# Twelve seven-product pairs instead of ten in the down projection, three of them with weight sums made during the up projection

## The chip, the core and the metric

The kernel runs on one core of a Trainium2 chip. The time is the device time of one execution in microseconds (us). Of this kernel before the change there are three timed runs, 1303.25 to 1303.45 us, median 1303.36, and one further execution taken with the profiler. The engines have short names below: PE multiplies matrices, DVE and ACT work element by element, POOL and SP only issue transfers in the stages that matter here.

## The reference

One layer of an encoder trunk on 256 positions with a width of 2048, all in float32. The change is in the last part, the gated feed-forward network with 5504 hidden channels:

```python
def conv_ffn(x, g_norm, w_up, conv_k, conv_b, w_down):
    h = rms_norm(x, g_norm)
    up = h @ w_up
    ...
    up = (pad[:, :t] * conv_k[0] + pad[:, 1:t + 1] * conv_k[1]
          + pad[:, 2:t + 2] * conv_k[2] + conv_b)
    gate, val = jnp.split(up, 2, axis=-1)
    return x + (jax.nn.silu(gate) * val) @ w_down
```

Ahead of it stand the two mixer branches, their merge and an output projection; behind it a last RMS norm.

## The kernel before

**Precision.** PE gets each float32 operand as a high and a low part. A weight piece is loaded as `wraw`, ACT copies its rounded high part to `whi` (L153), and DVE subtracts it to get the low part `wlo` (L154). This is called a split below. A product of two split operands is three matmuls, high by high, low by high, high by low; `triple` writes them (L291 to L293).

**Order of work.** The weights are a list of pieces. `begin(i)` stands ahead of the matmuls of piece i: it issues loads up to piece i + 4 (five `wraw` buffers), the splits up to piece i + 3 (four `whi` and `wlo` buffers), and then the tasks that `at(i, ...)` left for piece i. Every engine takes its own instructions in the written order, and semaphores do the rest.

**Up projection.** A group is eight pieces of 256 contraction rows by 512 columns: the columns are two blocks of 128 gate channels and two of the matching value channels. PE runs 64 matmuls with `whi` (L205) and 64 with `wlo` (L209) for it. While the next group runs, `ev_up` adds the two halves of each result bank (`tb`, `ta`), makes the convolution and the gate, and splits the result into the activation tile `a`. Two blocks of 128 channels form one contraction pair of the down projection, so group p leaves pair p. There are 21 whole pairs and a last single block.

**Down projection.** It runs twice, for columns 0 to 1023 (g = 0) and 1024 to 2047 (g = 1), each with 43 pieces of 128 rows by 1024 columns. Two pieces are a pair q. A plain pair takes eight triples: two row blocks, two column blocks, two halves of the contraction. For the pairs in `DOWN_QUADS` a scheme with seven products is used instead (`run_wide`): three triples at the first piece (r = 0) and four at the second (r = 1), with sums of weight blocks and sums of activation blocks as operands. The four weight sums, `t13` and `t24`, are made by four DVE additions (`weight_sums`, at piece i - 3 for a pair that begins at piece i) and split at i - 2 (`weight_sums_split`: two ACT copies, two DVE subtractions into `h13`, `l13`, `h24`, `l24`). The split sums have two sets of buffers that take turns, one in `hpool`, one in a pool `twice` (`both_rooms`). The activation sums of a pair are made while the up projection runs, `sums` and `sums_split` of `ev_up`, stored to device memory by POOL (L1029), and read back by `stored` at piece i - 4 (L1194) into one of two buffers.

Ten pairs per g are such pairs: pairs 3, 5, 7, 9, 10, 12, 14, 16, 17 and 19 of the contraction, which stand at those places for g = 0 and at 2, 4, 6, 8, 9, 11, 13, 14, 16 and 18 for g = 1. The seven-product pair needs whole `wraw` pieces for its sums, but of its own two pieces only one and a half are split.

**Tail.** The last four pieces of g = 1 are run block by block, so that the final norm and the stores of one block lie beside the products of the next.

Of the kernel before, what the change touches and what calls it, by code (L numbers as in the profile page):

```python
# [8 lines left out]
F32 = mybir.dt.float32  # L9
# [48 lines left out]
TURN_X2 = (13, 1)  # L58
Y_GAP = 224
PAD = 16  # L60
DOWN_PAIRS = (3, 5, 7, 9, 10, 12, 14, 16, 17, 19)
DOWN_QUADS = (DOWN_PAIRS, (2, 4, 6, 8, 9, 11, 13, 14, 16, 18))


@with_exitstack
def trunk_kernel(ctx, tc, x, x_t, vecs, w_in, ln_g, ln_b, w_st, b_s, rpb, w_branch, w_out, w_up, w_down,
# [17 lines left out]
    wpool = keep("weights")  # L84
    tmp = keep("tmp")
    hpool = keep("hT")
    ypool, y_st = pool("yT", "right")

    junk = tmp.tile([128, 512], F32, name="junk")
# [17 lines left out]
        return first  # L107

    raw, split_t = {}, {}
    whole, units = {}, {}  # L110
    n_loaded = [0]
    n_split = [0]

    def load_to(n):
        while n_loaded[0] < min(n, len(pieces)):
            i = n_loaded[0]
            n_loaded[0] += 1
            if i in preload:
                for f in preload[i]:
                    f()  # L120
            src, r0, kn, (c0, cn, nb, cs), step = pieces[i]
            w = wpool.tile([128, 2, 512], F32, name="wraw", bufs=LOAD_AHEAD)
# [15 lines left out]
            raw[i] = w  # L138
            if i in whole:
                whole[i] = w  # L140
# [31 lines left out]
    def at(i, f):  # L172
        tasks.setdefault(i, []).append(f)
# [90 lines left out]

    def wide(src, row0, order, c0, acts, quads, room, done, sums=None, stored=None, split_room=None):
        n0 = plan_wide(src, row0, order, c0)
        boxes = {}
        for q in quads:  # L270
            i = n0 + 2 * q
            own = split_room or room
            whole[i] = whole[i + 1] = None
            units[i], units[i + 1] = 1, 2
            b = boxes[q] = {}
            if stored:
                b["acts"] = {}
                at(i - 4, lambda b=b, k=order[2 * q]: stored(k // 2, b["acts"]))
            else:
                b["acts"] = sums[order[2 * q]]  # L280
# [51 lines left out]
    def weight_sums_split(box, room):  # L332
        u = []
        for name, t in zip(("13", "24"), box.pop("w")):
            h, l = room("h" + name, F32R), room("l" + name, F32R)
            nc.scalar.activation(h, t, AF.Copy)  # L336
            nc.vector.tensor_sub(l, t, h.bitcast(F32))
            u.append((h, l))
        box["t"] = {1: [x[:, 0] for x in u[0]], 3: [x[:, 1] for x in u[0]],
                    2: [x[:, 1] for x in u[1]], 4: [x[:, 0] for x in u[1]]}  # L340

# [282 lines left out]
    def combine(ps):  # L624
        outs = []
        bs = []
        for p in ps:
            t = tmp.tile([128, T], F32, name="tb", bufs=3)
            nc.scalar.activation(t, p[:, T:], AF.Copy)
            a = tmp.tile([128, T], F32, name="ta", bufs=6)  # L630
            nc.vector.tensor_add(a, p[:, :T], t)
            outs.append(a)
        return outs
# [353 lines left out]
    def ev_up(f0, nb):  # L987
        def done(ps, i):
            n = nb
            a = []  # L990
            own = {}
            for p in ps:
                t = tmp.tile([128, T], F32, name="tb", bufs=3)
                nc.scalar.activation(t, p[:, T:], AF.Copy)
                u = tmp.tile([128, T], F32, name="ta", bufs=6)
                nc.vector.tensor_add(u, p[:, :T], t)
                a.append(u)

            def conv(b):
                c = []  # L1000
                for u, ch in ((a[b], f0 + b), (a[n + b], NF + f0 + b)):
                    nc.vector.tensor_mul(u, u, rs["rb"])  # L1002
                    v = ff["p"].tile([128, T], F32, name="tc", bufs=4)
                    nc.scalar.activation(v, u, AF.Identity, scale=ck[:, 1, ch:ch + 1], bias=ck[:, 3, ch:ch + 1])  # L1004
                    c.append((u, v, ch))
                for u, v, ch in c:
                    nc.vector.scalar_tensor_tensor(v[:, 1:], u[:, :T - 1], ck[:, 0, ch:ch + 1], v[:, 1:],  # L1007
                                                   op0=OP.mult, op1=OP.add)
                    nc.vector.scalar_tensor_tensor(v[:, :T - 1], u[:, 1:], ck[:, 2, ch:ch + 1], v[:, :T - 1],
                                                   op0=OP.mult, op1=OP.add)  # L1010
# [173 lines left out]
    def down_room(name, dt):  # L1184
        return hpool.tile([128, 2, 512], dt, name=h_room[name])

    def both_rooms(name, dt):
        n = ff[name] = ff.get(name, -1) + 1
        return (ff["twice"] if n % 2 else hpool).tile([128, 2, 512], dt, name=h_room[name])

    def stored(pair, box):
        n = ff["turn"] = ff.get("turn", -1) + 1
        o = down_room(f"s{n % 2}", F32R)
        nc.gpsimd.dma_start(o.bitcast(F32), ff["kept"][pair])  # L1194
        box["s"] = sums_of(o)

    def down_order(g):
        free = [p for p in range(NF // 2) if p not in DOWN_PAIRS]
# [2 lines left out]
        return tuple(2 * p + kk for p in pairs for kk in range(2)) + (NF - 1,)  # L1201

    g_dn = [wide(w_d, 0, down_order(g), g * 1024, lambda k: ff["a"][k], DOWN_QUADS[g], down_room,
                 (ev_sums(2 * g, down_room), ev_down if g == 0 else finish), stored=stored, split_room=both_rooms) for g in range(2)]
    ff["kept"] = {p: dram.tile([128, 2, 512], F32, name=f"sums{p}") for p in DOWN_PAIRS}

    first_chunk = X_TURN[1][0]
    preload[2] = [lambda: load_xt(2 * first_chunk, 1)]
# [85 lines left out]
    s_room["st"].close()  # L1294
    for half in (1, 0):
        mg["m_st", half].close()
    fa, fa_st = pool("act")
    ctx.push(fa_st)
    ff["ap"] = [fa.tile([128, min(2, NF - k), 2, T], F32R, name=f"a{k // 2}") for k in range(0, NF, 2)]
    ff["a"] = [ff["ap"][k // 2][:, k % 2] for k in range(NF)]  # L1300
    ff["more"], more_st = pool("more")
    fc = {}

# [5 lines left out]
        run_group(g)  # L1309
    def open_twice():  # L1310
        more_st.close()
        ff["twice"], twice_st = pool("twice")
        ctx.push(twice_st)

# [60 lines left out]
```

## Time and profile before

| | |
|---|---|
| median of three runs | 1303.36 us |
| profiled execution | 1303.95 us, its span 1302.2 us |
| granted clock of PE | 0.999 of full speed |
| busy: PE, DVE, ACT, POOL | 99%, 83%, 60%, 8% |
| DMA | 280.34 MB, mean 215 GB/s |
| first matmul of the down projection | 1073.20 us from the span's start |

The time and the span of the profiled execution differ by 1.75 us, which lie outside the profile. A row of a timeline has the start, the duration, the engine, the line and the operation, out<-in, and in brackets how long the engine stood idle just before and what ended that. Rows in time order can be merged (x and a count). The rows of grouped instructions have the busy time and the mean duration in ns behind the bar. PE's matmuls overlap: a row's duration is longer than the distance from one start to the next.

### The profile page before, as it was taken

To read this page: it belongs to the slowest core of one execution; us is meant where nothing else is said; L and a number is where in the kernel's file an instruction comes from. 1 tells how busy PE (TensorE), PEld (TensorE's weight loads), DVE (VectorE), ACT (ScalarE), POOL (GpSimd) and SP (SyncE) were. 2 spreads that over 40 slices of the span, in tenths; PEclk is the share of its full clock that TensorE was granted. 3 is DMA by queue.
4 is the path that set the end of the run, shared out by engine and by line. 5 is a ranking of instruction groups with operands and counts; after the bars stand their busy time and mean duration, and the time that the engine had idled before them with its cause. 6 is when DMAs were issued, how large, how long until landed. Compare 5 with 4: busy or idle time off the path is not lost.

```text
span 1302.2 us, 19268 instructions
## 1 busy us (share of the span) xinstructions
PE 1291.6 (99%) x6703; PEld 1102.0 (85%) x6703; DVE 1078.2 (83%) x1620; ACT 780.2 (60%) x1156; POOL 108.9 (8%) x212
## 2 busy tenths in 40 slices
PE   9999999999999999999999999999999999999997
PEld 7888888888888888888888888888888888888886
DVE  7896777677689988997778878787878889999997
ACT  7765576676655645566555556565655656655564
POOL 0006405413000000000000000000000000000000
PEclk9999999999999999999999999999999999999999
DMA  9789656566566667665566666666666658876883
GB/s 368 268 275 251 199 164 210 178 165 191 178 213 224 200 188 249 202 212 173 172 202 196 189 213 196 210 195 216 188 211 200 211 157 293 292 268 222 271 285 112
DMA packets 174513, 280.34 MB, mean 215 GB/s; under 512 B 13392, under 2 KB 121552, under 8 KB 174416
## 3 DMA queue, kind: packets, MB, share of 16 engines
q1 hardware_dynamic: 164944, 251.89, 60.1%
q0 software_dynamic: 8896, 26.17, 6.5%
q8 instruction: 52, 0.85, 0.3%
q10 hardware_dynamic: 576, 1.06, 0.2%
q14 instruction: 45, 0.37, 0.1%
HBM read 268.05 MB, written 8.91 MB: 213 GB/s over the span
## 4 chain that ended last, share of the span: by engine, by line
PE 99%; DVE 1%; ACT 0%; issue 0%; POOL 0%; POOLq 0%; ACTq 0%
PE bank L205 31%; PE bank L209 16%; PE bank L291 12%; PE bank L293 12%; PE bank L292 12%; PE bank L233 4%; PE bank L234 4%; PE bank L235 4%; PE bank L777 1%; PE bank L827 0%; PE bank L906 0%; PE bank L642 0%; PE bank L978 0%; PE bank L817 0%; PE bank L450 0%
## 5 line engine op out<-in xcount | busy, mean ns | idle before, releaser
L154 DVE TENSOR_TENSOR wlo<-wraw,whi 128x1024 fp32r<-128x1024 f32 (+1 forms) x472 | 545.4, 1170 | 174.1 <-ACT whi L153 93.1
L153 ACT ACTIVATE whi<-wraw 128x1024 fp32r<-128x1024 f32 (+1 forms) x472 | 470.0, 1009 | 213.0 <-PE bank L292 75.2
L205 PE MATMUL bank<-h,whi 128*128 128x512 f32 x1760 | 425.8, 392 | 0.6 <-DVE ya L646 0.6
L205 PEld LDWEIGHTS bank<-h,whi 128*128 128x128 f32 x1760 | 322.0, 188 | 62.7 <-DVE ya L646 1.0
L209 PEld LDWEIGHTS bank<-h,wlo 128*128 128x128 f32 x1760 | 225.9, 191 | 8.8
L209 PE MATMUL bank<-h,wlo 128*128 128x256 f32 x1760 | 228.6, 283 | 0.0
L1004 ACT ACTIVATE tc<-ta,ck 128x256 f32<-128x256 f32 x86 | 47.1, 594 | 117.1 <-DVE ta L1002 117.1
L293 PE MATMUL bank<-wlo,a 128*128 128x512 f32 x224 | 87.3, 390 | 0.0
L292 PE MATMUL bank<-whi,a 128*128 128x512 f32 x224 | 87.2, 389 | 0.0
L291 PE MATMUL bank<-whi,a 128*128 128x512 f32 x224 | 87.1, 389 | 0.0
L291 PE MATMUL bank<-whi,h 128*128 128x512 f32 x210 | 82.2, 391 | 0.0
L293 PE MATMUL bank<-wlo,h 128*128 128x512 f32 x210 | 82.1, 391 | 0.0
L292 PE MATMUL bank<-whi,h 128*128 128x512 f32 x210 | 81.8, 389 | 0.0
L336 ACT ACTIVATE h<-h 128x1024 fp32r<-128x1024 f32 x40 | 40.2, 1053 | 34.3 <-DVE h L328 34.3
L1007 DVE SCALAR_TENSOR_TENSOR tc<-ta,ck,tc 128x255 f32<-128x255 f32 x86 | 41.4, 481 | 14.5 <-ACT tc L1004 14.5
L1029 POOL DMA_DIRECT2D sums<-so x10 | 5.4, 538 | 548.1 <-DVE so L494 459.8
L233 PE MATMUL bank<-whi,y 128*128 128x512 f32 x128 | 50.5, 394 | 0.0
L233 PE MATMUL bank<-whi,h 128*128 128x512 f32 x128 | 50.4, 394 | 0.0
L235 PE MATMUL bank<-wlo,h 128*128 128x512 f32 x128 | 49.9, 390 | 0.0
L235 PE MATMUL bank<-wlo,y 128*128 128x512 f32 x128 | 49.9, 390 | 0.0
L234 PE MATMUL bank<-whi,h 128*128 128x512 f32 x128 | 49.8, 389 | 0.0
L234 PE MATMUL bank<-whi,y 128*128 128x512 f32 x128 | 49.8, 389 | 0.0
(285 smaller groups left out, 1833.2 us busy)
## 6 DMA issues: line engine op xcount, KB each, us to landing
wraw<-in_w_up_dram SPq DMA_DIRECT2D x336, 256.0 KB, 3.2
wraw<-in_w_in_dram SPq DMA_DIRECT2D x111, 512.0 KB, 4.6
wraw<-in_w_down_dram SPq DMA_DIRECT2D x86, 512.0 KB, 5.3
wraw<-in_w_in_dram SPq DMA_DIRECT2D x66, 256.0 KB, 3.3
wraw<-in_w_branch_dram SPq DMA_DIRECT2D x32, 512.0 KB, 4.5
wraw<-in_w_out_dram SPq DMA_DIRECT2D x32, 512.0 KB, 4.5
h<-sums POOLq DMA_DIRECT2D x20, 512.0 KB, 6.4
sums<-so POOLq DMA_DIRECT2D x10, 512.0 KB, 4.2
```

Source lines behind the costliest of these rows:

```text
L153: nc.scalar.activation(h[:, k, :m], w[:, k, :m], AF.Copy)
L154: nc.vector.tensor_sub(l[:, k, :m], w[:, k, :m], h[:, k, :m].bitcast(F32))
L205: nc.tensor.matmul(p, h[:, k - k0, b * 128:(b + 1) * 128], acts(k), start=k == 0, stop=k == nk - 1)
L209: nc.tensor.matmul(p[:, :T], l[:, k - k0, b * 128:(b + 1) * 128], acts(k)[:, 0, :], start=False, stop=False)
L233: nc.tensor.matmul(p, xh, h[:, kk, :m], start=st, stop=False)
L234: nc.tensor.matmul(p, xl, h[:, kk, :m], start=False, stop=False)
L235: nc.tensor.matmul(p, xh, l[:, kk, :m], start=False, stop=sp)
L291: nc.tensor.matmul(p, xh, h, start=st, stop=False)
L292: nc.tensor.matmul(p, xl, h, start=False, stop=False)
L293: nc.tensor.matmul(p, xh, l, start=False, stop=sp)
L1004: nc.scalar.activation(v, u, AF.Identity, scale=ck[:, 1, ch:ch + 1], bias=ck[:, 3, ch:ch + 1])
L1007: nc.vector.scalar_tensor_tensor(v[:, 1:], u[:, :T - 1], ck[:, 0, ch:ch + 1], v[:, 1:], op0=OP.mult, op1=OP.add)
```

## The change

Two more pairs of each half use seven products, twelve in place of ten. The lists of places are new: 3, 5, 6, 7, 9, 11, 12, 13, 15, 17, 18, 19 for g = 0 and 2, 4, 5, 6, 8, 10, 11, 12, 14, 16, 17, 18 for g = 1.

For the pairs 6, 12 and 18 the weight sums are not made in the down projection. `split_ahead` makes them during the up projection, once for each pair and g, so six times, beginning at the groups 2, 5, 9, 11, 15 and 17: POOL loads the 1 MB of weights at the first piece of that group into `tw`, DVE makes the four additions at its last two pieces and at the first two of the next group, and ACT and DVE split the sums at the third and fifth piece of the next group. The high parts go through the buffer `so`, which the activation sums also use and of which there is one; the low parts replace the sums in `tw`. POOL stores the four tiles of 512 KB to device memory. In the down projection `split_read` reads the four tiles back, at piece i - 6, into one set of buffers in `twice`. Such a pair makes no sums in the down projection, and of its first weight piece only half the columns are loaded.

The nine other pairs of each half make their split sums in `hpool` alone, in one set of buffers. The activation sums have a third buffer, `s2`, in `twice`. The tiles `ta` and `tb` move from the pool `tmp`, open for the whole kernel, to pools of their own, the second of which closes ahead of `twice` and lies where `twice` comes to lie.

```diff
-DOWN_PAIRS = (3, 5, 7, 9, 10, 12, 14, 16, 17, 19)
-DOWN_QUADS = (DOWN_PAIRS, (2, 4, 6, 8, 9, 11, 13, 14, 16, 18))
+DOWN_PAIRS = (3, 5, 6, 7, 9, 11, 12, 13, 15, 17, 18, 19)
+DOWN_QUADS = (DOWN_PAIRS, (2, 4, 5, 6, 8, 10, 11, 12, 14, 16, 17, 18))
+SPLIT_PAIRS = (6, 12, 18)
+SPLIT_IN = ((2, 5), (9, 11), (15, 17))
...
+            if i in halved:
+                kn = 1
...
+            if split and k // 2 in SPLIT_PAIRS:
+                halved.add(i)
+                at(i - 6, lambda b=b, k=k: split(k // 2, b))
+                continue
+            whole[i] = whole[i + 1] = None
             at(i - 3, lambda i=i, b=b: weight_sums(i, b, room))
-            at(i - 2, lambda b=b, own=own: weight_sums_split(b, own))
+            at(i - 2, lambda b=b: weight_sums_split(b, room))
...
-    def both_rooms(name, dt):
-        n = ff[name] = ff.get(name, -1) + 1
-        return (ff["twice"] if n % 2 else hpool).tile([128, 2, 512], dt, name=h_room[name])
-
     def stored(pair, box):
-        n = ff["turn"] = ff.get("turn", -1) + 1
-        o = down_room(f"s{n % 2}", F32R)
+        n = ff["turn"] = (ff.get("turn", -1) + 1) % 3
+        o = ff["twice"].tile([128, 2, 512], F32R, name="s2") if n == 2 else down_room(f"s{n}", F32R)
         nc.gpsimd.dma_start(o.bitcast(F32), ff["kept"][pair])
         box["s"] = sums_of(o)
+
+    def split_read(g):
+        def read(pair, box):
+            u = []
+            for n in ("13", "24"):
+                u.append([ff["twice"].tile([128, 2, 512], F32R, name=p + n) for p in "hl"])
+                for t, src in zip(u[-1], t_kept[pair, g][n]):
+                    nc.gpsimd.dma_start(t.bitcast(F32), src)
+            split_sums(box, u)
+        return read
+
+    def split_ahead(pair, g, i):
+        box = {}
+
+        def load():
+            w = box["w"] = ff["more"].tile([128, 4, 512], F32, name="tw")
...
+        def add(d, a, b):
+            w = box["w"]
+            nc.vector.tensor_add(w[:, d], w[:, a], w[:, b])
+
+        def split(c, n):
+            w = box["w"][:, c:c + 2]
+            h = ff["more"].tile([128, 2, 512], F32R, name="so")
+            low = w.bitcast(F32R)
+            nc.scalar.activation(h, w, AF.Copy)
+            nc.vector.tensor_sub(low, w, h.bitcast(F32))
+            for dst, v in zip(t_kept[pair, g][n], (h.bitcast(F32), w)):
+                nc.gpsimd.dma_start(dst, v)
+
+        at(i, load)
+        for n, (d, a, b) in enumerate(((0, 0, 1), (1, 1, 3), (3, 0, 3), (2, 2, 3))):
+            at(i + 6 + n, lambda d=d, a=a, b=b: add(d, a, b))
+        at(i + 10, lambda: split(0, "13"))
+        at(i + 12, lambda: split(2, "24"))
...
+    turns["p"], turns_st = pool("turns2")
     ff["more"], more_st = pool("more")
...
     def open_twice():
         more_st.close()
+        turns_st.close()
         ff["twice"], twice_st = pool("twice")
```

The first place is DVE in the up projection, from the second piece's split on after group 11 has ended. The kernel before has there:

```order
L154 TENSOR_TENSOR wlo_8814<-wraw_8791,whi_8813 128x1024
L1002 TENSOR_TENSOR ta_8777<-ta_8777,rb_6196 128x256
L1002 TENSOR_TENSOR ta_8785<-ta_8785,rb_6196 128x256
L1007 SCALAR_TENSOR_TENSOR tc_8818<-ta_8777,ck_88,tc_8818 128x255
L1009 SCALAR_TENSOR_TENSOR tc_8818<-ta_8777,ck_88,tc_8818 128x255
L1007 SCALAR_TENSOR_TENSOR tc_8821<-ta_8785,ck_88,tc_8821 128x255
L1009 SCALAR_TENSOR_TENSOR tc_8821<-ta_8785,ck_88,tc_8821 128x255
L154 TENSOR_TENSOR wlo_8855<-wraw_8810,whi_8854 128x1024
L1015 TENSOR_TENSOR tc_8818<-tc_8818,tc_8821 128x256
```

The changed kernel has at that place, on DVE, where `tw` holds the weights of one pair ahead and `so` their high parts:

```order
L1227 TENSOR_TENSOR tw_8647<-tw_8647 128x512
L160 TENSOR_TENSOR wlo_8900<-wraw_8876,whi_8899 128x1024
L1227 TENSOR_TENSOR tw_8647<-tw_8647 128x512
L1015 TENSOR_TENSOR ta_8862<-ta_8862,rb_6229 128x256
L1015 TENSOR_TENSOR ta_8870<-ta_8870,rb_6229 128x256
L1020 SCALAR_TENSOR_TENSOR tc_8905<-ta_8862,ck_91,tc_8905 128x255
L1022 SCALAR_TENSOR_TENSOR tc_8905<-ta_8862,ck_91,tc_8905 128x255
L1020 SCALAR_TENSOR_TENSOR tc_8908<-ta_8870,ck_91,tc_8908 128x255
L1022 SCALAR_TENSOR_TENSOR tc_8908<-ta_8870,ck_91,tc_8908 128x255
L160 TENSOR_TENSOR wlo_8942<-wraw_8896,whi_8941 128x1024
L1234 TENSOR_TENSOR tw_8647<-tw_8647,so_8945 128x1024
L1028 TENSOR_TENSOR tc_8905<-tc_8905,tc_8908 128x256
```

Two additions and the subtraction of a split ahead (L1227, L1234) stand between the splits of the up projection's own pieces (L160, L154 before) and the convolution.

The second place is POOL at the start of the down projection. The kernel before reads the activation sums of pairs 3 and 5, two parts of the last norm's weight, and the sums of pairs 7 and 9:

```order
L1194 DMA h6_11135<-sums3_123 128x1024
L1194 DMA h7_11231<-sums5_124 128x1024
L1329 DMA gfin_11237<-in_norm_final_dram 128x512
L1329 DMA gfin_11239<-in_norm_final_dram 128x512
L1194 DMA h6_11328<-sums7_125 128x1024
L1194 DMA h7_11413<-sums9_126 128x1024
```

The changed kernel has on POOL there:

```order
L1203 DMA h6_11282<-sums3_126 128x1024
L1203 DMA h7_11379<-sums5_127 128x1024
L1212 DMA h13_11381<-h13_6_0_138 128x1024
L1212 DMA l13_11382<-l13_6_0_139 128x1024
L1212 DMA h24_11385<-h24_6_0_140 128x1024
L1212 DMA l24_11386<-l24_6_0_141 128x1024
L1385 DMA gfin_11393<-in_norm_final_dram 128x512
L1385 DMA gfin_11395<-in_norm_final_dram 128x512
L1203 DMA s2_11448<-sums6_128 128x1024
L1203 DMA h6_11486<-sums7_129 128x1024
```

The four tiles of pair 6 (L1212) and its activation sums have come in ahead of the sums of pair 7.

More of the change, by code (lines that the diff above doesn't have):

```diff
@@ L86, in trunk_kernel @@
     hpool = keep("hT")
+    turns, turns_st = pool("turns")
+    turns = {"p": turns}
     ypool, y_st = pool("yT", "right")
@@ L109, in trunk_kernel @@
     raw, split_t = {}, {}
-    whole, units = {}, {}
+    whole, units, halved = {}, {}, set()
     n_loaded = [0]
@@ L262, in run_group, with wide @@
             done(ps, b)
-    def wide(src, row0, order, c0, acts, quads, room, done, sums=None, stored=None, split_room=None):
+    def wide(src, row0, order, c0, acts, quads, room, done, sums=None, stored=None, split=None):
         n0 = plan_wide(src, row0, order, c0)
@@ L271, in wide @@
             i = n0 + 2 * q
-            own = split_room or room
-            whole[i] = whole[i + 1] = None
+            k = order[2 * q]
             units[i], units[i + 1] = 1, 2
@@ L277, in wide @@
                 b["acts"] = {}
-                at(i - 4, lambda b=b, k=order[2 * q]: stored(k // 2, b["acts"]))
+                at(i - 4, lambda b=b, k=k: stored(k // 2, b["acts"]))
             else:
-                b["acts"] = sums[order[2 * q]]
+                b["acts"] = sums[k]
+            if split and k // 2 in SPLIT_PAIRS:
[3 more added lines that the diff above has]
+            whole[i] = whole[i + 1] = None
             at(i - 3, lambda i=i, b=b: weight_sums(i, b, room))
-            at(i - 2, lambda b=b, own=own: weight_sums_split(b, own))
+            at(i - 2, lambda b=b: weight_sums_split(b, room))
         return ("wide", n0, order, acts, quads, boxes, done)
@@ L627, in combine @@
         for p in ps:
-            t = tmp.tile([128, T], F32, name="tb", bufs=3)
+            t = turns["p"].tile([128, T], F32, name="tb", bufs=3)
             nc.scalar.activation(t, p[:, T:], AF.Copy)
-            a = tmp.tile([128, T], F32, name="ta", bufs=6)
+            a = turns["p"].tile([128, T], F32, name="ta", bufs=6)
             nc.vector.tensor_add(a, p[:, :T], t)
@@ L992, in done @@
             for p in ps:
-                t = tmp.tile([128, T], F32, name="tb", bufs=3)
+                t = turns["p"].tile([128, T], F32, name="tb", bufs=3)
                 nc.scalar.activation(t, p[:, T:], AF.Copy)
-                u = tmp.tile([128, T], F32, name="ta", bufs=6)
+                u = turns["p"].tile([128, T], F32, name="ta", bufs=6)
                 nc.vector.tensor_add(u, p[:, :T], t)
@@ L1203, in trunk_kernel @@
     g_dn = [wide(w_d, 0, down_order(g), g * 1024, lambda k: ff["a"][k], DOWN_QUADS[g], down_room,
-                 (ev_sums(2 * g, down_room), ev_down if g == 0 else finish), stored=stored, split_room=both_rooms) for g in range(2)]
+                 (ev_sums(2 * g, down_room), ev_down if g == 0 else finish), stored=stored, split=split_read(g)) for g in range(2)]
     ff["kept"] = {p: dram.tile([128, 2, 512], F32, name=f"sums{p}") for p in DOWN_PAIRS}
+    t_kept = {}
+    for p, turn in zip(SPLIT_PAIRS, SPLIT_IN):
+        for g in range(2):
+            t_kept[p, g] = {n: [dram.tile([128, 2, 512], F32, name=f"{h}{n}_{p}_{g}") for h in "hl"]
+                            for n in ("13", "24")}
+            split_ahead(p, g, g_up[turn[g]][1])
     first_chunk = X_TURN[1][0]
```

6 lines of the change are left out of this document (added).

## The prediction

> **What bounds the kernel now.** I read the page first, then the waits of PE's weight loads, then a table of stages.
>
> ```profile
> PE 1291.6 (99%) x6703; PEld 1102.0 (85%) x6703; DVE 1078.2 (83%) x1620; ACT 780.2 (60%) x1156; POOL 108.9 (8%) x212
> PE 99%; DVE 1%; ACT 0%; issue 0%; POOL 0%; POOLq 0%; ACTq 0%
> PEld bank L293 <- DVE wlo L154: 0.3, 1, 0.3
> 706.31:1020.00 313.69, 313.69 (x1802) 277.12 (x1801) 254.88 (x436) 184.36 (x291) 4.82 (x9) 1.00 0.65 203
> 1080.00:1280.00 200.00, 200.00 (x884) 165.62 (x883) 190.96 (x228) 119.17 (x136) 11.72 (x22) 1.00 0.78 264
> ```
>
> The first two lines are the page's busy times and its chain of waits: both are PE. The third is the whole list of PE's waits in the down projection, one wait of 0.3 us for DVE. The last two are stages of the up and the down projection: length, busy time of PE, its loads, DVE, ACT and POOL, granted clock, DMA share, GB/s. DVE is busy 254.88 of 313.69 us (81%) in the first and 190.96 of 200 us (95%) in the second. So PE sets the time everywhere, but in the down projection DVE is almost a second bound, and an edit that only added seven-product pairs would soon be DVE's.
>
> How fast PE goes there is seen in the timeline, with the stage's first and last matmul around one triple:
>
> ```profile
> 1073.20 0.39 PE L291 MATMUL bank<-whi,a 128*128 128x512 f32 x1
> ...
> 1104.00 0.39 PE L291 MATMUL bank<-h,a 128*128 128x512 f32 x1
> 1104.23 0.39 PE L292 MATMUL bank<-h,a 128*128 128x512 f32 x1
> 1104.46 0.39 PE L293 MATMUL bank<-h,a 128*128 128x512 f32 x1
> 1104.68 0.39 PE L291 MATMUL bank<-whi,a 128*128 128x512 f32 x1
> ...
> 1293.52 0.39 PE L293 MATMUL bank<-wlo,a 128*128 128x512 f32 x1
> ```
>
> A triple starts every 0.68 us (1104.68 - 1104.00), a matmul every 0.227, though each row lasts 0.39. By the code there are 2 x (10 x 7 + 11.5 x 8) = 324 triples, 220.3 us; the rows give 1293.52 + 0.23 - 1073.20 = 220.5. So nothing but issue is in this stage, and what follows it, the tail to 1302.2, is 8.5 us.
>
> **PE's saving.** Each new seven-product pair drops one triple. Two more per half are four triples, 12 matmuls: 4 x 0.68 = 2.72 us. That is all the change can take from this path; nothing that it removes elsewhere was waited for.
>
> **DVE in the down projection.** Its costs, by form, in the stage's groups:
>
> ```profile
> L154 DVE TENSOR_TENSOR wlo<-wraw,whi 128x1024 fp32r<-128x1024 f32 x61 | 73.3, 1221 | 7.6 <-ACT whi L153 7.6
> L337 DVE TENSOR_TENSOR h<-h,h 128x1024 fp32r<-128x1024 f32 x40 | 47.1, 1221 | 0.0
> L327 DVE TENSOR_TENSOR h<-h,wraw 128x512 f32<-128x512 f32 x20 | 13.8, 692 | 0.7
> L154 DVE TENSOR_TENSOR wlo<-wraw,whi 128x512 fp32r<-128x512 f32 x20 | 13.8, 688 | 0.2 <-ACT whi L153 0.2
> ```
>
> The other three additions are taken like L327, 0.69 us. A pair with its sums made here costs 4 x 0.69 + 2 x 1.22 + 1.22 + 0.69 = 7.11 us of DVE against 7 x 0.68 = 4.76 of PE; a plain pair 2.44 against 5.44; a pair that is read back 1.91 against 4.76. From place 3 to 19 of the first half, before: DVE 10 x 7.11 + 7 x 2.44 = 88.2, PE 85.7. After: 9 x 7.11 + 3 x 1.91 + 5 x 2.44 = 81.9, PE 12 x 4.76 + 5 x 5.44 = 84.3. DVE goes from behind PE to ahead of it, and two costly pairs are never neighbours any more. Price: 0.
>
> **One set of buffers.** The copies of the next costly pair must now wait for PE's last product of the one before. The timeline has both, for the pairs at places 12 and 14:
>
> ```profile
> 1139.82 0.39 PE L293 MATMUL bank<-h,a 128*128 128x512 f32 x1
> 1140.19 2.01 ACT L336 ACTIVATE h<-h 128x1024 fp32r<-128x1024 f32 x2 [1.83 <-DVE h L328]
> ```
>
> With two sets, ACT already begins only when the last of these matmuls is ending, held by DVE's sums; behind it on ACT are the splits of the next pieces. At worst the wait adds about 0.02 us to that start (1139.82 + 0.39 - 1140.19), and PE gets to these sums 7.5 us later (two plain pieces and r = 0, 11 triples). Below nothing it cannot go, since PE was not waiting; above, the 7.5 less ACT's 1.05 and DVE's 2.44 leave some 4 us of cover. Price 0.
>
> **Reading back.** 2 x 3 x 4 tiles of 512 KB come in on POOL's queue beside the weights. The tightest place is the first, pair 6:
>
> ```profile
> 1083.56 0.48 DVE L1009 SCALAR_TENSOR_TENSOR tc<-ta,ck,tc 128x255 f32<-128x255 f32 x1
> 1098.85 2.35 DVE L337 TENSOR_TENSOR h<-h,h 128x1024 fp32r<-128x1024 f32 x2
> 1101.96 0.39 PE L291 MATMUL bank<-h,h 128*128 128x512 f32 x1
> 1102.97 0.63 ACT L153 ACTIVATE whi<-wraw 128x512 fp32r<-128x512 f32 x1 [1.83 <-DMA wraw<-in_w_down_dram]
> 1076.00:1084.00 8.00, 8.00 (x36) 6.41 (x35) 7.59 (x15) 5.37 (x10) 0.00 (x0) 1.00 1.01 400
> 1084.00:1090.00 6.00, 6.00 (x28) 4.95 (x28) 5.97 (x10) 3.66 (x6) 1.08 (x2) 1.00 0.76 244
> 1090.00:1106.00 16.00, 16.00 (x72) 13.27 (x71) 15.78 (x19) 9.17 (x11) 1.07 (x2) 1.00 0.82 274
> h<-sums POOLq DMA_DIRECT2D x20, 512.0 KB, 6.4
> ```
>
> The tiles lie where `ta` lay, so they start when the last convolution has read it, 1084.05. PE wants them at 1104.68 + 2.04 = 1106.7. In those 22 us DMA moved 6 x 244 + 16 x 274 = 5.85 MB; new are 4 x 0.524 + 0.524 (the sums of pair 6) - 0.262 (the half piece) = 2.36 MB: 8.2 MB. At 400 GB/s, which the stage just ahead shows at a full DMA share, 22 us carry 8.8 MB. It fits, but at first in a heap: if the 2.36 and 0.5 MB of the norm's weight come within 11 us beside 270 GB/s of weights, about 1.1 MB are left over, 2.7 us by which a weight piece is late. ACT waits for a piece there already (1.83). Cover: the low parts of pair 5 begin at 1098.85, the first is done at 1100.07 and PE needs it at 1101.96 + 0.45: 2.3 us; and a piece is requested several us ahead of its split. Nothing can be gained, since PE has no wait there; lost can be 2.7 - 2.3 = 0.4 us, and 0.4 + 0.68 at pair 7, whose products now begin a triple earlier: 1.5 us. I take 0, since the pieces' own lead comes on top of the cover. The later reads start as soon as the previous read-back pair is done, some ten pieces ahead, where DVE is no tighter.
>
> The row for capacity is 400 GB/s. The Trainium skill, HBM Reference, Specifications, gives about 425 GB/s for a core that streams alone and 358 for its share when both cores of a pair do. By 358 the 22 us would carry 7.9 MB, 0.3 MB too few, under 1 us late; one core runs here and the row is above that share, so the trace speaks for the first figure.
>
> **The up projection.** Six times DVE gets 4 x 0.69 + 2 x 1.22 = 5.2 us, ACT 2 x 1.05, POOL one load and four stores. The stage has 59 us of DVE idle in the 314 above, against 31 in all; what counts is one group. For one, DVE's idle places, ACT's splits, and PE's high products (12, then 7 behind the low ones, one every 0.23 us):
>
> ```profile
> 818.91 1.23 DVE L154 TENSOR_TENSOR wlo<-wraw,whi 128x1024 fp32r<-128x1024 f32 x1 [0.47 <-ACT whi L153]
> 821.95 1.23 DVE L154 TENSOR_TENSOR wlo<-wraw,whi 128x1024 fp32r<-128x1024 f32 x1 [1.81 <-PE bank L209]
> 837.74 1.23 DVE L154 TENSOR_TENSOR wlo<-wraw,whi 128x1024 fp32r<-128x1024 f32 x1 [0.54 <-PE bank L209]
> ...
> 824.54 1.05 ACT L153 ACTIVATE whi<-wraw 128x1024 fp32r<-128x1024 f32 x1
> ...
> 830.42 1.04 ACT L153 ACTIVATE whi<-wraw 128x1024 fp32r<-128x1024 f32 x1
> ...
> 831.68 1.04 ACT L153 ACTIVATE whi<-wraw 128x1024 fp32r<-128x1024 f32 x1
> ...
> 833.78 2.91 PE L205 MATMUL bank<-h,whi 128*128 128x512 f32 x12
> ...
> 838.44 1.78 PE L205 MATMUL bank<-h,whi 128*128 128x512 f32 x7
> ```
>
> The group's last piece has its high part at 831.46, and PE begins with it after eight of the 12, at 835.62: 4.2 us of cover. The next group's first piece has 832.72 against 838.44 + 4 x 0.23 = 839.36: 6.6 us. Of the change, DVE does one addition in the group's first piece and one in its second, 1.22 us in its third and fifth. The first addition falls into the 1.81 us. The second addition and the first subtraction push the convolution, and ACT, which waits for it, by 0.69 + 1.22 = 1.9 us: 2.3 us of cover are left. The second copy and subtraction come behind the last piece's split and before the next one, which is later by 1.9 + 1.05 = 3.0 us: 3.6 us left. The lag of about 3 us meets 0.54 us of idle in the same group and 0.47 + 1.81 in the following, so it is nearly gone before the next time. The added activation sums of pairs 6, 11, 13, 15 and 18 in place of 10, 14 and 16 sit where the unchanged kernel has them every other group. POOL waits for its stores with nothing urgent behind it. Price on PE: 0; if the cover were gone, every further us would count six times.
>
> **Sum.** 1303.95 - 2.72 = 1301.23 us for the profiled execution, whose span becomes 1299.5. It lies 0.59 us over the median of the runs, 1303.36; from that median the forecast is 1303.36 - 2.72 = 1300.64, so 1300.6 us. A difference of 0.2%, 2.6 us, is about what a measurement of this kernel can tell from no change; the forecast is just over it.
>
> **Rivals.** *Transfers in the down projection.* The four reads of pair 6 may go one behind the other: 4 x 6.4 = 25.6 us from 1084.05 is 1109.7, 3.0 us after PE wants them; or the weights beside them come late by more than the 2.3 us above. For it speaks ACT's wait of 1.83 us for a weight piece at this very place and the heap of 1.1 MB; against it that 400 GB/s of DMA were seen with POOL's reads in flight, so that reads overlap. One such stall takes between 0.3 and 3.0 us off the saving: 1300.9 to 1303.7 us. Later reads have more lead.
>
> *ACT waits for the store out of `so`, and the kernel gets slower.* The second copy of a split ahead overwrites `so`, whose first contents must have landed in device memory. ACT works in order, and the splits of the weights stand behind this copy. The landing times, of the stores on the page and of stores and reads together by tile:
>
> ```profile
> sums<-so POOLq DMA_DIRECT2D x10, 512.0 KB, 4.2
> DMA to landing us min/median/max: 3.3/5.6/9.9
> ```
>
> In the group above the first copy would end near 826.6 us (824.54 and two copies of 1.05), its store be issued by 827.2 and land at 831.4 with 4.2 us; the second copy is due at 831.46 + 1.9 = 833.4. With 9.9 us it lands at 837.1, ACT stands for 3.7 us, and the next group's first high part is ready at 833.4 + 3.7 + 1.05 + 0.4 + 1.04 = 839.6, 0.2 us late. So the rival decides from about 9.7 us of landing, and each us beyond costs 6 us in all: slower than before from 10.2 us, by 0.2% from 10.6; at 11.2 us the loss is 6 x 1.5 = 9.0, and the time 1303.36 - 2.72 + 9.0 = 1309.6 us. For it: the low part's store of 512 KB follows at once on the same queue, so two are in flight beside weights at 203 GB/s. Against it: the median is under half of what is needed, and 1.05 MB of stores and 1.2 MB of weights within 6 us are 375 GB/s, still below 400. The Trainium skill, DMA: Bandwidth & Descriptors, Anatomy of one DMA, gives a transfer from POOL's queue as 2.0 us plus its bytes over 436 GB/s, 3.2 us for 512 KB, most of the fixed part being the receipt of the last write, longest for device memory. The rows of this case are longer, and the stores' 4.2 us are shorter than the reads' 6.4, so the trace does not show stores as the slow kind; by the page's 3.2 us this rival would have nothing.
>
> That the 12 matmuls would not go is no rival, since PE's order is fixed by the lists.
>
> **How the numbers follow.** Forecast 0.55; the transfers in the down projection 0.30; the wait for `so` 0.15. The three runs lie 0.2 us apart and the forecast only 0.1 us beyond the bound, so of its 0.55 I count 0.43 as faster by over 0.2% and 0.12 as within. The first rival is within with 0.28, and slower with 0.02 if several places stall; the second is slower with 0.13 and within with 0.02. Faster 0.43, same 0.42, slower 0.15. The range begins at 1300.3 (the one wait of 0.3 us for DVE may go too) and goes to 1304.0, the first rival's end and the runs' spread; the second rival is left out.
>
> **What would show it.** Right: first matmul of the down projection still at 1073.2, a triple every 0.68 us, last matmul at 1290.8, DVE's busy share of the down projection a few per cent lower, that of the up projection near 90%. The first rival: PE idle near 1102 to 1113 behind `h` or a late `wraw`. The second: the first matmul of the down projection later than 1073.2, and ACT idle before the copy into `so`, ended by a DMA. If PE's triple were longer than 0.68 us, or the tail longer than 8.5 us, a cause is at work that is not among these.

## The result, and the profile after

The changed kernel takes 1300.82 us (median of 20 runs, 1300.41 to 1302.92), the kernel before 1303.34 us (20 runs beside it, 1302.94 to 1304.95). That is 2.52 us or 0.19% less; the recorded comparison of all these runs gives a ratio of 0.9984 (the medians alone 0.9981), with an interval of 0.9977 to 0.999. The profiled execution took 1300.74 us. Forecast was 1300.6.

The page of the changed kernel, with its busy times and the shares of its chain:

```profile
PE 1288.4 (99%) x6691; PEld 1100.1 (85%) x6691; DVE 1096.7 (84%) x1654; ACT 786.0 (61%) x1166; POOL 141.6 (11%) x272
PE 98%; DVE 0%; DMA 0%; ACT 0%; issue 0%
```

There are 12 matmuls less, 34 DVE and 10 ACT operations more, and the chain is still PE's. Where the time went is read from three matmul starts: the first of the up projection, the first of the down projection, the last of all. The row of before:

```profile
592.19 0.62 PE L205 MATMUL bank<-h,whi 128*128 128x512 f32 x2
```

Those of the changed kernel:

```profile
591.46 1.30 PE L211 MATMUL bank<-h,whi 128*128 128x512 f32 x5
1072.47 0.39 PE L301 MATMUL bank<-whi,a 128*128 128x512 f32 x1
1290.24 0.39 PE L303 MATMUL bank<-wlo,a 128*128 128x512 f32 x1
```

| stage | before, us | after, us |
|---|---|---|
| up to the first up matmul | 592.19 | 591.46 |
| up projection | 481.01 | 481.01 |
| down projection, first to last start | 220.32 | 217.77 |
| from there to the end of the span | 8.68 | 8.66 |

The up projection, which now carries the added work, has not moved by a hundredth. The down projection is 2.55 us shorter. The 0.73 us at the top lie ahead of the up projection. Of the change, the first load of `tw`, which POOL issues at 510.15 us, and the new place of `ta` and `tb` fall there. Over the nine profiles of this study that start moves between 591.2 and 593.8 us: 591.24 to 593.83 in the six kernels with that load, 591.49 to 592.19 in the three without it. So I take the 0.73 us for spread, and the medians' 2.52 us for the down projection's 2.55. The two windows of the prediction, for the changed kernel (columns as there):

```profile
706.31:1020.00 313.69, 313.69 (x1803) 277.12 (x1802) 276.47 (x467) 190.73 (x300) 19.03 (x34) 1.00 0.78 253
1080.00:1280.00 200.00, 200.00 (x884) 165.60 (x883) 182.78 (x220) 114.42 (x133) 25.80 (x49) 1.00 0.88 328
```

DVE went from 81% to 88% in the up projection and from 95% to 91% in the down projection, and PE is busy without a gap in both.

### The profile page after: what moved, and what is told of

Read it like the earlier page. It is cut to its first block, busy times and chain, and to the rows that moved or that the text cites. A ratio compares the mean times of both kernels' runs of the same rounds, so it can differ in the third digit from the quotient of the medians.

```text
span 1298.9 us, 19474 instructions
## 1 busy us (share of the span) xinstructions
PE 1288.4 (99%) x6691; PEld 1100.1 (85%) x6691; DVE 1096.7 (84%) x1654; ACT 786.0 (61%) x1166; POOL 141.6 (11%) x272
## 4 chain that ended last, share of the span: by engine, by line
PE 98%; DVE 0%; DMA 0%; ACT 0%; issue 0%
PE bank L211 31%; PE bank L215 16%; PE bank L301 12%; PE bank L303 12%; PE bank L302 12%; PE bank L239 5%; PE bank L240 4%; PE bank L241 4%; PE bank L790 1%; PE bank L840 0%; PE bank L919 0%; DMA wraw<-in_w_in_dram 0%; PE bank L655 0%; PE bank L830 0%; PE bank L991 0%; ACT whi L159 0%
## 5 line engine op out<-in xcount | busy, mean ns | idle before, releaser
L160 DVE TENSOR_TENSOR wlo<-wraw,whi 128x1024 fp32r<-128x1024 f32 (+1 forms) x472 | 543.3, 1164 | 151.8 <-ACT whi L159 102.4
L301 PE MATMUL bank<-whi,h 128*128 128x512 f32 x206 | 80.6, 391 | 0.4 <-ACT whi L159 0.4
L302 PE MATMUL bank<-whi,h 128*128 128x512 f32 x206 | 80.4, 390 | 0.0
L303 PE MATMUL bank<-wlo,a 128*128 128x512 f32 x200 | 77.9, 390 | 0.0
L301 PE MATMUL bank<-whi,a 128*128 128x512 f32 x200 | 77.8, 389 | 0.0
L302 PE MATMUL bank<-whi,a 128*128 128x512 f32 x200 | 77.8, 389 | 0.0
L346 ACT ACTIVATE h<-h 128x1024 fp32r<-128x1024 f32 x36 | 36.2, 1053 | 25.0 <-DVE h L338 15.8
L239 PE MATMUL bank<-whi,h 128*128 128x512 f32 x128 | 50.4, 394 | 0.0
L240 PE MATMUL bank<-whi,h 128*128 128x512 f32 x128 | 49.8, 389 | 0.0
L301 PEld LDWEIGHTS bank<-whi,h 128*128 128x128 f32 x206 | 38.8, 188 | 8.7 <-ACT whi L159 0.8
```

The lines of the kernel that those rows point to most:

```text
L160: nc.vector.tensor_sub(l[:, k, :m], w[:, k, :m], h[:, k, :m].bitcast(F32))
L239: nc.tensor.matmul(p, xh, h[:, kk, :m], start=st, stop=False)
L240: nc.tensor.matmul(p, xl, h[:, kk, :m], start=False, stop=False)
L301: nc.tensor.matmul(p, xh, h, start=st, stop=False)
L302: nc.tensor.matmul(p, xl, h, start=False, stop=False)
L303: nc.tensor.matmul(p, xh, l, start=False, stop=sp)
```

## The experiments

Seven kernels, compared with the kernel before, which took 1303.28 us beside the first four and 1303.26 beside the others. My theory: the gain is the 12 matmuls and nothing else; the sums made ahead are needed because DVE could not make two more per half; one set of buffers, reading back and the work in the up projection are hidden. The rivals: relief of DVE or of the transfers itself brings or costs time; the read-back or the store out of `so` is close to being waited for.

**Ten pairs per half, three of them read back.** The matmuls of before, the rest of the change as it is:

```
-DOWN_PAIRS = (3, 5, 6, 7, 9, 11, 12, 13, 15, 17, 18, 19)
-DOWN_QUADS = (DOWN_PAIRS, (2, 4, 5, 6, 8, 10, 11, 12, 14, 16, 17, 18))
+DOWN_PAIRS = (3, 5, 6, 9, 11, 12, 15, 17, 18, 19)
+DOWN_QUADS = (DOWN_PAIRS, (2, 4, 5, 8, 10, 11, 14, 16, 17, 18))
```

> Ten seven-product pairs per half again, three of them read back (places 3, 5, 6, 9, 11, 12, 15, 17, 18, 19; seven with sums made in the down projection). Theory (the time is PE's and the whole gain is the 12 matmuls): 4 x 0.68 = 2.72 us more than the changed kernel, so the kernel before's 1303.3 us within 0.3, with no PE wait in the down projection, though DVE is relieved and the transfers are there. Rival (relieving DVE is worth something by itself): below 1302.7 us. Rival (the transfers cost): above 1304.

Measured: 1303.72 us (11 runs), ratio 1.0003 (0.9994 to 1.0012), and 220.35 us for the down projection against 220.32 before. The median is 0.44 us above the kernel before, a little outside the 0.3 of the expectation; the interval contains no change, and the stage has not moved. Its window there:

```profile
1080.00:1280.00 200.00, 200.00 (x884) 165.67 (x883) 164.36 (x193) 108.22 (x125) 24.28 (x46) 1.00 0.88 321
```

DVE fell from 95% to 82% busy and the time did not move: DVE was never waited for in before. Nor do the transfers and stores, the third buffer `s2` and the moved pools, all of which this kernel has too, cost anything that this can show. What is left for the gain are the two pairs per half.

**Twelve pairs per half, all sums made in the down projection.** The matmuls of the change, nothing read back, both sets of buffers again:

```
-SPLIT_PAIRS = (6, 12, 18)
-SPLIT_IN = ((2, 5), (9, 11), (15, 17))
+SPLIT_PAIRS = ()
+SPLIT_IN = ()
...
-            at(i - 2, lambda b=b: weight_sums_split(b, room))
+            at(i - 2, lambda b=b: weight_sums_split(b, both_rooms if split else room))
...
```

(behind the dots, `both_rooms` of the kernel before comes back)

> The changed kernel's twelve places per half, but all 24 pairs make their sums in the down projection, in two sets of buffers; nothing is made ahead. Theory (DVE was almost the bound, so more pairs need the sums made ahead): from place 3 to 19 DVE has 12 x 7.11 + 5 x 2.44 = 97.5 us by durations (about 88 where starts are 0.61 apart) against PE's 84.3, so 4 to 13 us too much per half, of which some 7 us of lead are used up first: PE waits for wlo and for the sums, 2 to 8 us in all, and the time is 1302.5 to 1308 us, centre 1304. Rival (lead and overlap hide it, and the split ahead was not needed): 1300.8 us as the changed kernel.

Measured: 1312.4 us (5 runs), ratio 1.0073 (1.006 to 1.0086): slower by 9.1 us, and above the expected range. The window and PE's waits in the down projection:

```profile
1080.00:1280.00 200.00, 193.67 (x847) 158.09 (x846) 197.06 (x242) 116.60 (x137) 13.82 (x26) 1.00 0.77 267
PEld bank L303 <- DVE wlo L160: 13.2, 10, 2.4
```

DVE is at 99% and PE waits ten times for a low part of a weight piece. The down projection takes 229.51 us instead of 217.77, so 11.7 us go to these waits. This shows that the split ahead is what makes the two pairs affordable: DVE, free of charge in the kernel before, becomes the bound with two more pairs per half.

**One set of buffers alone,** in the kernel before:

```
-                 (ev_sums(2 * g, down_room), ev_down if g == 0 else finish), stored=stored, split_room=both_rooms) for g in range(2)]
+                 (ev_sums(2 * g, down_room), ev_down if g == 0 else finish), stored=stored, split_room=down_room) for g in range(2)]
```

> The kernel before with one set of buffers for the split sums instead of two, nothing else. Theory (the copies find PE done with the pair before): 1303.3 us within 0.3. Here two costly pairs are neighbours at places 9 and 10, 16 and 17, where the wait is real: up to 2.7 us each for ACT and DVE, hidden by a cover of 4 us. Rival (the second set was needed): PE waits at the neighbours, 1304 to 1307 us.

Measured: 1303.66 us (11 runs), ratio 1.0002 (0.9993 to 1.0011); 220.36 us for the down projection, so the 0.38 us of the median lie elsewhere. From the list of waits of this kernel:

```profile
ACT h L336 <- PE bank L292: 10.5, 8, 2.3
PEld bank L293 <- DVE wlo L154: 0.3, 1, 0.3
```

ACT does wait for PE's products, the eight times of the first row and twice more for L293, up to 2.3 us, which it did not before; PE's one wait is what it was. The wait is real and entirely hidden.

**One pair more: thirteen per half, four read back.** If the theory holds, there is more to be had:

```
-DOWN_PAIRS = (3, 5, 6, 7, 9, 11, 12, 13, 15, 17, 18, 19)
-DOWN_QUADS = (DOWN_PAIRS, (2, 4, 5, 6, 8, 10, 11, 12, 14, 16, 17, 18))
-SPLIT_PAIRS = (6, 12, 18)
-SPLIT_IN = ((2, 5), (9, 11), (15, 17))
+DOWN_PAIRS = (3, 5, 6, 7, 9, 10, 11, 13, 14, 15, 17, 18, 19)
+DOWN_QUADS = (DOWN_PAIRS, (2, 4, 5, 6, 8, 9, 10, 12, 13, 14, 16, 17, 18))
+SPLIT_PAIRS = (6, 10, 14, 18)
+SPLIT_IN = ((2, 4), (6, 8), (10, 12), (14, 16))
```

> One more step the same way: thirteen seven-product pairs per half, four of them (6, 10, 14, 18) made ahead in eight passes at groups 2, 4, 6, 8, 10, 12, 14 and 16 and read back. Theory (PE sets the time and has cover): two triples fewer, 1.36 us less than the changed kernel, 1299.4 us. Rival (transfers become the bound, 0.37 of full rate and more in the changed kernel's down projection, now 2.36 MB more per half): PE waits for weights, above 1300.8 us.

Measured: 1299.55 us (9 runs), ratio 0.9974 (0.9964 to 0.9983), the fastest kernel of this study; 1299.4 was expected. The down projection takes 216.27 us: 220.32 less six triples of 0.68 is 216.24. Its two windows and the one wait of PE:

```profile
706.31:1020.00 313.69, 313.69 (x1803) 277.15 (x1802) 287.71 (x485) 196.24 (x307) 24.92 (x45) 1.00 0.83 274
1080.00:1280.00 200.00, 200.00 (x884) 165.63 (x883) 181.71 (x221) 114.49 (x133) 31.11 (x59) 1.00 0.92 350
PEld bank L303 <- DVE wlo L160: 0.3, 1, 0.3
```

DVE at 92% of the up projection and DMA at 350 GB/s in the down projection still hide everything. The rival of this run falls: with 22 GB/s more than in the changed kernel, PE waits for nothing more. (The 0.37 of full rate in the expectation is not what the profile has: the DMA share is 0.88 in the changed kernel's window and 0.92 here.)

**One pair more in the first half alone,** a fourteenth, its sums made in the down projection:

```
-DOWN_PAIRS = (3, 5, 6, 7, 9, 10, 11, 13, 14, 15, 17, 18, 19)
-DOWN_QUADS = (DOWN_PAIRS, (2, 4, 5, 6, 8, 9, 10, 12, 13, 14, 16, 17, 18))
+DOWN_PAIRS = (3, 5, 6, 7, 9, 10, 11, 13, 14, 15, 17, 18, 19, 4)
+DOWN_QUADS = ((3, 5, 6, 7, 9, 10, 11, 13, 14, 15, 17, 18, 19, 20), (2, 4, 5, 6, 8, 9, 10, 12, 13, 14, 16, 17, 18))
...
-        free = [p for p in range(NF // 2) if p not in DOWN_PAIRS]
-        kept = list(DOWN_PAIRS)
+        kept = list(DOWN_PAIRS[:len(DOWN_QUADS[g])])
+        free = [p for p in range(NF // 2) if p not in kept]
```

(against the kernel with thirteen)

> The kernel with thirteen pairs and four read back, with one pair more in the first half alone (pair 4, at place 20, sums made in the down projection). Theory: one triple fewer, 0.68 us less than that kernel, if DVE's lead at the border of the halves (7 to 9 us) carries the extra 4.7 us beside the sums and additions that end the first half: 1298.9 us and a down projection of 215.6 us from first to last matmul. Rival (DVE is the bound there): PE waits for wlo at the start of the second half, and the time is 1299.6 us or more.

Measured: 1303.05 us (11 runs), ratio 0.9997 (0.9988 to 1.0006). The theory missed here and the rival was right. The down projection takes 218.64 us, where 216.27 less 0.68 would be 215.6: 3.0 us are lost. PE's three longest waits between 1160 and 1230 us, around the border of the halves (a fourth has 0.2 us):

```profile
PEld bank L303 <- DVE wlo L160: 2.4, 1, 2.4
PEld bank L301 <- DVE h L940: 0.7, 1, 0.7
PEld bank L301 <- DVE x L937: 0.3, 1, 0.3
```

At the border DVE also has the additions of the half just finished (L937 to L941), and a costly pair right ahead of them comes on top. One pair too many there loses more than four triples bring. The limit of this path is DVE at one place, with 184.59 of 200 us (92%) busy in the usual window, less than the 95% of the kernel before. The stage explains 2.4 of the 3.5 us by which the median lies above the kernel with thirteen. What the rest is, no trace here shows; in five of the eleven executions the mean granted clock is 0.996 or 0.997, in the profiled one 0.998, so PE's clock behind these waits, as in the last section, is a guess.

**The split ahead, stored twice and thrice.** For the second rival of the prediction, ACT's wait for the store out of `so`: in the changed kernel, one or two more copies of the first store ahead of the real ones, so that `so` comes free later.

```
+            if n == "13":
+                for _ in range(1):
+                    nc.gpsimd.dma_start(t_kept[pair, g][n][0], h.bitcast(F32))
```

(`range(2)` in the second kernel)

> The changed kernel, with the first high part of each split ahead stored twice, one after the other, out of so, so that so comes free later. In the changed kernel's profile the first store is issued 0.5 us after the copy (826.93), the second copy into so starts without a wait (832.34), and PE would stand still if it started after about 836.3, that is 9.4 us after the first store's issue. Two stores in a row should take 8 to 9 us: ACT waits about 3 us six times, PE not at all, 1300.8 us. Rival (ACT's wait reaches PE sooner, since DVE and ACT lag together): 1302 to 1310 us.

> The same with three stores in a row, 12 to 13 us, over the 9.4 us. Theory: each of the six passes holds ACT some 7 us and PE about 3 us, 18 us in all: 1312 to 1322 us, centre 1319, all of it as PE's wait for whi or wlo in the up projection. Rival (the lead of three split pieces is larger than reckoned): under 1303 us.

Measured with one more: 1300.86 us (10 runs), ratio 0.998 (0.9971 to 0.9989), up projection 481.01 us. With two more: 1328.16 us (4 runs), ratio 1.0192 (1.0178 to 1.0205), up projection 509.98 us: the place and the direction were expected, 6 us above the range were not. The waits, with one more store:

```profile
ACT so L1233 <- DMA h<-so: 15.3, 6, 2.9
PEld bank L303 <- DVE wlo L160: 0.4, 1, 0.4
```

With two more:

```profile
ACT so L1233 <- DMA h<-so: 40.7, 6, 7.3
PEld bank L211 <- ACT whi L159: 21.2, 7, 4.3
```

By the prediction's group, ACT may stand for about 3.5 us before PE notices (3.7 us cost 0.2). Up to 2.9 us cost nothing; a mean of 40.7 / 6 = 6.8 us costs PE six waits and a short seventh, and 6 x (6.8 - 3.5) = 19.8 us is near the 21.2 of the list. So the rival's mechanism exists, and its 3.5 us fit both runs; the changed kernel, without the extra stores, has no such wait at all. The rest of the 28.97 us is in the last section.

## Why the prediction was right

**PE's saving.** Right: 2.72 us forecast, 2.55 in the stage and 2.52 in the medians. Most of the missing 0.17 is one step at the start of the down projection, on PE's timeline:

```profile
1075.20 0.39 PE L301 MATMUL bank<-whi,a 128*128 128x512 f32 x1
1075.43 0.39 PE L302 MATMUL bank<-whi,a 128*128 128x512 f32 x1
1075.84 0.50 PE L303 MATMUL bank<-wlo,a 128*128 128x512 f32 x1
```

1075.84 - 1075.43 is 0.41, where a matmul otherwise starts after 0.23: PE waits for a low part (in the list of waits 0.4 us, before 0.3). The same step took 0.28 us before (1076.16 to 1076.44), so it accounts for 0.13. I had let the range begin lower because this wait might go; it grew a little instead. With thirteen pairs, where the list again says 0.3 and the step takes 0.27, 4.05 of six triples' 4.08 us arrived. Why the wait is longer in the changed kernel I have not settled.

**DVE in the down projection.** Right: 91% instead of 95%, and "near 90%" in the up projection is 88%. That it mattered was argued, and the kernel with twelve pairs made here shows it. The prices behind it were too high. I had added up durations, and DVE's rows overlap as PE's do. In the kernel with twelve pairs made here, where DVE has no idle time between these rows, the first additions of three costly pairs show the distance:

```profile
1101.10 0.68 DVE L336 TENSOR_TENSOR h<-wraw 128x512 f32<-128x512 f32 x1
1107.63 0.68 DVE L336 TENSOR_TENSOR h<-wraw 128x512 f32<-128x512 f32 x1
1116.44 0.68 DVE L336 TENSOR_TENSOR h<-wraw 128x512 f32<-128x512 f32 x1
```

From the first to the second lies one costly pair, 6.53 us instead of 7.11; from the second to the third a costly and a plain one, 8.81, so a plain one is 2.28 instead of 2.44. By these the kernel before needs 10 x 6.53 + 7 x 2.28 = 81.3 us of DVE against 85.7 of PE, 95%: DVE was not behind PE, as the prediction had it, but just ahead, which fits that PE did not wait for it. The price of 0 stood all the same. Twelve pairs made here need 12 x 6.53 + 5 x 2.28 = 89.8 us against 84.3, 5.5 too many in a half; PE lost 11.7 us over both halves, about twice that, though not evenly: its listed waits are 3.8 us up to 1180 us and 9.4 behind, so a lead covered some of the first half's excess. The 7 us of lead per half in that run's expectation are more than this leaves room for; the 88 us that it named for starts 0.61 us apart were near.

**One set of buffers.** Right: price 0. A size within it was not: I had reckoned the wait at 0.02 us, from one place. In the changed kernel ACT waits five times for PE here, four times up to 1.9 us and once, as the second half begins, 3.9, just within the 4 us of cover (from ACT's waits in the down projection, with the one for weight pieces that the next paragraph needs):

```profile
ACT whi L159 <- DMA wraw<-in_w_down_dram: 23.4, 19, 2.9
ACT h L346 <- PE bank L303: 5.3, 4, 1.9
ACT h L346 <- PE bank L302: 3.9, 1, 3.9
```

**Reading back.** The price, 0, was right; sizes within it were not. ACT waits 23.4 us in all for weight pieces (6.9 before), once 2.9 us, and the tightest place is where I had put it. Its rows in the changed kernel, with the reads' median times to landing and the 22 us of the estimate:

```profile
1095.25 1.07 ACT L159 ACTIVATE whi<-wraw 128x1024 fp32r<-128x1024 f32 x1 [2.85 <-DMA wraw<-in_w_down_dram]
1098.26 2.35 DVE L347 TENSOR_TENSOR h<-h,h 128x1024 fp32r<-128x1024 f32 x2
1101.40 0.39 PE L301 MATMUL bank<-h,h 128*128 128x512 f32 x1
...
h<-h POOLq DMA_DIRECT2D x12, 512.0 KB, 9.1
l<-l POOLq DMA_DIRECT2D x12, 512.0 KB, 11.1
...
1083.30:1105.30 22.00, 22.00 (x99) 18.22 (x98) 21.29 (x28) 12.74 (x15) 4.24 (x8) 1.00 1.01 377
```

ACT stood 2.85 us for a weight piece, and yet the sums of pair 5 are no later against PE (1098.26 with PE at 1101.40; before 1098.85 with 1101.96): the cover held. The 2.7 us that I had worked out for it are near this by luck, for the sum was wrong: 2.36 and 0.5 MB, less 11 us at 400 - 270 GB/s, leave 1.4 MB over, not 1.1, and that is 3.6 us. Two more terms were off. A read takes 9.1 to 11.1 us in the median of all places, not 6.4. And with the DMA share at 1.01 the 22 us moved 377 GB/s, 8.3 MB, not the 8.8 MB that 400 GB/s would give, where I had reckoned with 8.2.

The rival of four reads one behind the other did not come near, all the same. POOL issued the first of them at 1078.56 us, ahead of these 22 us, and the last at 1085.17; the four landed 4.9 to 9.1 us after their issue, so before 1095, and PE takes them up at 1106.16. The activation sums of pair 6 come last, with their time to landing and PE's first product with them:

```profile
1089.23 0.53 POOL L1203 DMA_DIRECT2D s<-sums  x1
DMA to landing us min/median/max: 10.1/10.1/10.1
1105.48 0.39 PE L301 MATMUL bank<-whi,s 128*128 128x512 f32 x1
```

They are there at about 1099.5, some 6 us early. Of the two figures of the Trainium skill (HBM Reference, Specifications), 425 GB/s for a core alone and 358 as its share, the measured 377 lies nearer the lower one; I had said the trace spoke for the upper. The 3.3 us ahead of these 22 moved 420 GB/s at a DMA share of 1.03, so what a full share carries differs here from one stretch to the next. The kernel with thirteen pairs sets this in proportion: 350 GB/s over 200 us and no wait of PE for any of it.

**The up projection.** Right. In group 10 of the changed kernel, on ACT and POOL:

```profile
825.37 1.04 ACT L1233 ACTIVATE so<-tw 128x1024 fp32r<-128x1024 f32 x1
831.39 1.04 ACT L159 ACTIVATE whi<-wraw 128x1024 fp32r<-128x1024 f32 x1
832.34 1.04 ACT L1233 ACTIVATE so<-tw 128x1024 fp32r<-128x1024 f32 x1
833.60 1.05 ACT L159 ACTIVATE whi<-wraw 128x1024 fp32r<-128x1024 f32 x1
...
h<-so POOLq DMA_DIRECT2D x12, 512.0 KB, 3.8
```

The last piece's high part is there at 831.39 + 1.04 = 832.43, 2.46 us before PE begins with it (2.3 forecast); the next group's first at 834.65, 4.0 us before PE's (3.6 forecast). The second copy into `so` waits for no store: these land in 3.8 us, where the rival needed 9.7. The kernel with one more store bears out that there was room.

**The chances.** Nearly as much was given to no measurable change as to faster. The bound between them was 0.2%; the result, 0.19% by the medians and 0.16% by the recorded ratio, lies just on the side of no measurable change, and the interval, 0.1 to 0.23%, leaves out zero but not the bound. So the forecast of the time held, while its being just over the bound was too fine a distinction for this measurement.

## What to carry to other kernels

Where one engine is busy without a gap, count what an edit takes from that engine, by the distance from one start to the next, and give it no credit for relief elsewhere: DVE's 95% in the kernel before cost nothing, and taking it to 82% brought nothing. But at 95% there is little room: two more pairs a half made DVE the bound, so work for it has to move to a stage where it has idle time; what limits the move then is the lead at single places (a copy's buffer, the border of two halves), which is worked out instruction by instruction and not from shares.

## What the runs showed of the hardware

An idle PE can cost more than its length, here at 2.63 us already. In the kernel with two more stores, the matmuls of the up projection behind each of its six waits, on PE's timeline (the idle time before each stands in brackets):

```profile
685.72 5.32 PE L211 MATMUL bank<-h,whi 128*128 128x512 f32 x16 [2.84 <-ACT whi L159]
756.85 5.50 PE L211 MATMUL bank<-h,whi 128*128 128x512 f32 x16 [2.63 <-ACT whi L159]
850.31 3.95 PE L211 MATMUL bank<-h,whi 128*128 128x512 f32 x16 [2.53 <-ACT whi L159]
899.49 5.53 PE L211 MATMUL bank<-h,whi 128*128 128x512 f32 x16 [3.89 <-ACT whi L159]
993.33 6.71 PE L211 MATMUL bank<-h,whi 128*128 128x512 f32 x16 [2.87 <-ACT whi L159]
1044.23 5.25 PE L211 MATMUL bank<-h,whi 128*128 128x512 f32 x16 [3.30 <-ACT whi L159]
```

The same 16 matmuls take 3.95 us behind an idle time of 2.53 us and 5.25 to 6.71 behind 2.63 us and more. The clock tells more. In this trace it changes at points that lie whole numbers of 3.41 us apart: the five drops begin at 685.31, 756.99, 900.35, 992.51 and 1043.71 us, 21, 42, 27 and 15 times 3.41 us from one to the next. Windows cut at these points, three around the first wait and three around the third, with PE's busy time behind the length and the granted clock in the third column from the end:

```profile
681.89:685.31 3.42, 0.99 (x5) 0.47 (x3) 0.86 (x1) 1.95 (x3) 0.53 (x1) 1.00 0.52 211
685.31:688.72 3.41, 3.00 (x7) 2.42 (x8) 3.41 (x6) 3.04 (x6) 0.53 (x1) 0.50 0.83 307
688.72:692.13 3.41, 3.41 (x21) 3.00 (x21) 2.94 (x6) 2.35 (x5) 0.00 (x0) 1.00 0.94 293
845.73:849.15 3.42, 2.06 (x14) 1.53 (x12) 0.11 (x1) 1.20 (x2) 0.00 (x0) 1.00 0.83 334
849.15:852.56 3.41, 2.25 (x10) 1.86 (x11) 3.41 (x5) 3.04 (x5) 1.07 (x2) 1.00 0.57 233
852.56:855.97 3.41, 3.41 (x24) 3.11 (x23) 3.34 (x7) 1.84 (x5) 0.00 (x0) 1.00 0.96 289
```

Ahead of each of the five drops PE was busy for 0.64 to 1.38 of the 3.41 us, and the next 3.41 us ran at 0.50 of full speed; behind the fifth wait of the rows above the clock stayed there for two such stretches (992.51 to 999.33). The third wait fell across one of the points, so that PE was busy for 2.06 and 2.25 us of the two stretches, and the clock stayed at 1.00. So it was not the length alone that told 2.53 from 2.63 us, but where the wait fell. This fits all six waits and is worked out from them alone.

One drop takes up to 0.50 x 3.41 = 1.7 us. Over all six waits, the idle times sum to 18.1 us, to which 6 x 0.16 us come since a row lasts 0.39 and the next matmul could start after 0.23: 19.0 us. The short seventh wait stretches the next row of 16 matmuls behind the third wait from 3.82 to 4.24 us, 0.4. The other 9.5 of the 28.97 us are the clock's: the five rows of 16 that ran in part at half speed are together 9.2 us longer than 3.82 each. That is the part that my expectation for this kernel left out. The Trainium skill (TensorE: Matmul & The Clock Gate, HAM oscillation — how this bites in real kernels) warns of PE idle for more than about 3.4 us; here 2.63 us already lowered the clock.
